# Hybrid SSD and attention layer: a gate vector turned on TensorE and loaded during the up projection, and another order of the last squares, means and scalings

## The chip, the cores and the metric

The kernel runs on one core of one Trainium2 chip. The metric is the time of one execution in microseconds on the device. The engines are named as in the profile: PE is TensorE (PEld its weight loads), DVE is VectorE, ACT is ScalarE, POOL is GpSimd, SP is SyncE. SP issues nearly all transfers in this kernel, and its queue is worked off in order: an issue that has to wait for a semaphore holds all issues behind it.

## The reference, cut to what matters

One layer over 512 latent tokens of width 1024 (and 256 context tokens, which only feed the mixers). The end of it is what the change touches:

```
x = x + gt1 * o_lat                                  # after the token mixer
x = x + gt2 * conv_ffn(modulate(x, norm2_g, sh2, sc2), ...)
return rmsnorm(x, final_g)                           # per token, times final_g per channel

def conv_ffn(h, w_up, conv_w, conv_b, w_down):
    u = dwconv_centred(h @ w_up, conv_w, conv_b)     # 1024 -> 2 x 2816
    return (silu(a) * b) @ w_down                    # 2816 -> 1024
```

gt2 is the last of six modulation vectors of 1024 values, computed from `silu(c) @ w_mod + b_mod`. It multiplies the output of the down projection channel by channel.

## The kernel before, in words

**Precision by three products.** Every weight and operand is split into a high part (whi, `S.copy` on ACT, L181) and a low part (wlo, a subtraction on DVE, L182), and every product is three matmuls (high x high, low x high, high x low). Weights come as pieces of 128 x 1024 values (512 KB), called keys: `load_raw` (L175) loads one to a buffer (tag raw, three of them, or dnraw, four), `split` makes the two parts in one of two buffers each of whi and wlo, or in dnw for two of every four down keys.

**The program.** `run` takes a list of steps with the keys that each needs, loads some keys ahead and emits the step. The instructions are then ordered on each engine by a list scheduler with costs of its own; it may emit an instruction well before its place in the program if what it needs is there. Inside `tc.manual_schedule` the named engines keep the written order. `weave(a, b)` spreads the entries of b evenly between those of a.

**Modulation turns.** The 32 `msteps` compute the modulation vectors beside other work: each scales and adds a weight piece on DVE into a tile tm, and each fourth one turns the sums on TensorE (L793) and adds up eighths of `mod2` (L795, L796). The last eight of them, `msteps[24:]`, are woven between the 22 steps of the up projection; mod2[:, 24:32] is the vector gt2.

**Up projection.** `up_step(t)`, t from 0 to 21, makes two products of 24 matmuls each and the convolution and gate on DVE and ACT. Beside the up steps, `x1_turn` turns the residual stream into rows by token (tiles te) and stores it to x1_d, and `x1_load` reads it back as rows: F["xt"].

**Row vectors.** `row_tiles` brings gt2 (half of it negated) and final_g to row form, so that every one of the 128 partitions holds the whole vector: gt2 lies in `g2c` as 128 partitions x 8, is stored to the DRAM tensor `g2_d` with the pattern "(c p) -> p c", and is read back with `partition_broadcast` into the two tiles rows_["g"]; final_g is read the same way into rows_["f"], whose second half is the tile tm. It is called at the first step of the down projection.

**Down projection.** Seven products, j = 0 to 6, of up to six steps u each, with operands fs of two halves; the weights of j = 1 to 4 are sums that were formed in DRAM earlier (dsum), those of j = 0, 5 and 6 come from wdn. Products 0, 2, 4 and 6 accumulate in two banks F["A"] (name mis), the others in acc. `BESIDE_DOWN` names what runs beside the steps: it forms the four output tiles from the products. The two upper ones (called far) are finished before the last step.

**The end.** The last step (`tail`) makes the product of tile 0, then that of tile 1 in two halves of 256 columns. For each tile and half, `near_last` multiplies by gt2 and adds the residual on DVE and sums the squares on ACT (`square_sum`, output to a buffer of tag ta, of which there are three; near_last takes another of them for its own product). `near_root` adds three partial means and takes the power -0.5: for tile 0 all on GpSimd, for tile 1 the addition on DVE (`mean_root`). `near_out` scales the columns 0 to 511 on ACT (already multiplied by final_g, tile p1, tag tb), scales the two halves of the columns 512 to 1023 on DVE, and issues the stores.

Of the kernel before, what the change touches and what calls it, by code (L numbers as in the profile page):

```python
# [9 lines left out]
F32 = mybir.dt.float32  # L10
F32R = mybir.dt.float32r
U8 = mybir.dt.uint8
AF = mybir.ActivationFunctionType
ALU = mybir.AluOpType
# [4 lines left out]
P = 128  # L19
# [5 lines left out]
NFF = 22  # L25
# [19 lines left out]
def tile_hybrid_layer(  # L45
# [31 lines left out]
    nc = tc.nc  # L77
    V, S, G, T = nc.vector, nc.scalar, nc.gpsimd, nc.tensor

    cpool = ctx.enter_context(tc.tile_pool(name="cpool", bufs=1))  # L80
# [26 lines left out]
    def accb():  # L107
        return bank("acc")

    def misb():  # L110
        return bank("mis")
# [3 lines left out]
    def tmp(tag):  # L115
        return tpool.tile([P, 512], F32, tag=tag, name=tag, bufs=TMP[tag])
# [24 lines left out]
    HC = D // 2  # L141
    DU = (DK + 1) // 2
    DSUMS = {i: dpool.tile([P, DK * HC], F32, name="dsum%d" % i) for i in (1, 2, 4, 5)}
    for j, t in enumerate((wdn[0], DSUMS[1], DSUMS[2], DSUMS[5], DSUMS[4], wdn[1], wdn[3])):
        for u in range(DU):
            n = min(2, DK - 2 * u) * HC
# [69 lines left out]
    def weave(a, b):  # L216
        r, n, m = [], len(a), len(b)
        for i in range(n):
            r.append(a[i])
            r += b[i * m // n : (i + 1) * m // n]  # L220
        return r
# [17 lines left out]
    ident = cpool.tile([P, P], F32, name="ident")  # L239
# [8 lines left out]
    phalf = cpool.tile([P, 4], F32, name="phalf")  # L248
# [15 lines left out]
    g2_d = dpool.tile([D], F32, name="g2_d")  # L264
# [154 lines left out]
    with tc.tile_pool(name="spool", bufs=1) as sp:  # L419
# [235 lines left out]
        r = {}  # L655
        cq = tmp("te")[:, :LC]
        for j in range(KT):
# [46 lines left out]
            x = ("hi", "lo") if j >= NU else ("hh", "hl")  # L704
# [31 lines left out]
        for n in range(2):  # L736
            for j in range(KT):
                x = ("hi", "lo") if j >= NU else ("hh", "hl")
# [131 lines left out]
    Q, F = {}, {}  # L870
# [775 lines left out]
    msteps = [m_step(i) for i in range(32)]  # L1646
    prog = proj_steps(0)
    for g in range(4):
        s = ssd_steps(g)
        f = fill[n2 + g : n2 + 1 + g]  # L1650
        b = proj_steps(g + 1) if g < 3 else fill[n2 + 4 : n3]
# [259 lines left out]
    def up_step(t):  # L1911
        def fn(wa, wb):
            pa, pb = accb(), accb()
            if t == 0:

                with tc.manual_schedule(engines={mybir.EngineType.PE}):
                    def product(ps, w, k, u):
                        c, z, st, en = slice(k * P, (k + 1) * P), HALF[u], u == 0 and k == 0, k == KT - 1
                        for v, y in ((0, h2h), (1, h2h), (0, h2l)):
                            T.matmul(  # L1920
                                ps[:, z], w[v][:, c], y[:, k, z],
                                start=st and v == 0 and y is h2h, stop=en and y is h2l, skip_group_check=True,
                            )

                    for k in range(KT):
                        norm2_k(k, 0)
                        if k == 2:
                            F["rs2"] = half_root(F["pf"], F["sq2"], 1)
                        if k == 5:
                            F["r2"].append(rms_spread(F["rs2"], 2))  # L1930
                        product(pa, wa, k, 0)
                        product(pb, wb, k, 0)
                    for k in range(KT):
                        norm2_k(k, 1)
                        product(pa, wa, k, 1)
                        product(pb, wb, k, 1)
                a = up_first(pa, pb, t)
            else:
                gemm([(pa, h2h, h2l)], wa)
                a = up_first(pa, pb, t)  # L1940
                gemm([(pb, h2h, h2l)], wb)
            up_second(a, pb, t)

        return [("up", t), ("up", NFF + t)], fn

    def x1_turn(c):

        def fn():
            t = tmp("te")
            V.transpose(t, x1[c // 4][:, c % 4, :])  # L1950
            for a in range(4):
                o = x1_d[:, c * P + 32 * a : c * P + 32 * a + 32].rearrange("(f i) j -> i f j", i=32)
                nc.sync.dma_start(o, t[32 * a : 32 * a + 32, :].rearrange("i (f j) -> i f j", j=32))

        return [], fn
# [10 lines left out]
    x1_rows = [], x1_load  # L1966
# [3 lines left out]
    rows_ = {}  # L1970

    def row_tiles():
        V.tensor_copy(g2c[:, 0:4], mod2[:, 24:28])
        V.tensor_scalar_mul(g2c[:, 4:8], mod2[:, 28:32], -1.0)
        nc.sync.dma_start(g2_d.rearrange("(c p) -> p c", p=P), g2c)
        tiles = [hpool.tile([P, HC], F32, tag=t, name="row" + t) for t in ("q2", "ssq", "rbc4")] + [tmp("tm")]
        rows_["g"], rows_["f"] = tiles[:2], tiles[2:]
        for i in range(2):
            z = slice(HC * i, HC * i + HC)
            nc.sync.dma_start(rows_["f"][i], fg_d[z].partition_broadcast(P))  # L1980
            nc.sync.dma_start(rows_["g"][i], g2_d[z].partition_broadcast(P))
# [9 lines left out]

        return F["xt"][h][:, i, HC * c + z.start : HC * c + z.stop]

    def square_sum(h, i, col_, x):
        sq = tmp("ta")[:, : x.shape[-1]]
        S.activation(sq, x, AF.Square, scale=1.0 / 32.0, accum_out=ss[:, 2 * h + i, col_ : col_ + 1])

    def scale_add(x, y, g, h, i, c):
# [37 lines left out]
    def mean_root(h, i, a, b, e):  # L2036
        ms, rs = (cpool.tile([P, 4], F32, tag=n, name=n, bufs=2)[:, 0:1] for n in ("ms", "rs"))
        V.scalar_tensor_tensor(ms, a, e, b, ALU.add, ALU.add)
        G.tensor_tensor(rs, ms, phalf[:, 0:1], ALU.pow)
        return rs  # L2040
# [26 lines left out]
    def near_last(i, b):  # L2067
        z, t = HALF[b], tmp("ta")[:, :HL]
        V.tensor_tensor(t, F["A"][i][:, z], rows_["g"][1][:, z], ALU.mult)
        x = xq(0, i, 1, z)  # L2070
        V.tensor_tensor(x, x, t, ALU.add)
        square_sum(0, i, 1 + b, x)

    def near_root(i):
        if i:
            F["near", i] = mean_root(0, i, ss[:, i, 1:2], ss[:, i, 2:3], ss[:, i, 0:1])
        else:
            ms, rs = (cpool.tile([P, 4], F32, tag=n, name=n, bufs=2)[:, 0:1] for n in ("ms", "rs"))
            G.tensor_tensor(ms, ss[:, i, 0:1], ss[:, i, 1:2], ALU.add)
            G.tensor_tensor(ms, ms, ss[:, i, 2:3], ALU.add)  # L2080
            G.tensor_tensor(rs, ms, phalf[:, 0:1], ALU.pow)
            F["near", i] = rs

    def near_out(i):
        rs, r = F["near", i], P * i
        S.activation(F["p1"][i], F["p1"][i], AF.Copy, scale=rs)
        (S if i else nc.sync).dma_start(out[r : r + P, 0:HC], F["p1"][i])
        for z in HALF:
            x = xq(0, i, 1, z)
            V.scalar_tensor_tensor(x, x, rs, rows_["f"][1][:, z], ALU.mult, ALU.mult)  # L2090
            if i or z.start:
                z = z if i else slice(0, HC)
                nc.sync.dma_start(out[r : r + P, HC + z.start : HC + z.stop], xq(0, i, 1, z))

    CHAIN = (0, 2, 4, 6)
    BESIDE_DOWN = {
        (0, 0): row_tiles, (1, 0): first_kept, (2, 0): fifth_kept, (3, 0): upper_sums, (4, 0): upper_put,
        (4, 4): lambda: far_done(0), (5, 0): lower_put, (5, 5): lambda: (far_done(1), far_roots()), (6, 0): near_put,
        (6, 1): lambda: far_out(0), (6, 2): lambda: far_out(1), (6, 3): near_done,
    }  # L2100
# [13 lines left out]
    def down_step(j, u):  # L2114
        tail = j == 6 and u == DU - 2

        def fn(*w):
            w = {u + n: x for n, x in enumerate(w)}
            if u == 0:
                if j == 0:  # L2120
                    F["A"] = [misb() for _ in TWO]
                F["ps", j] = F["A"] if j in CHAIN else [accb() for _ in TWO]
            ks = range(2 * u, DK if tail else min(2 * u + 2, DK))
            if tail:
                product(j, 0, w, ks)
                for z in HALF:
                    product(j, 1, w, ks, z)
                with tc.manual_schedule(engines={mybir.EngineType.DVE, mybir.EngineType.Activation}):
                    near_last(0, 0), near_last(0, 1)
                    near_root(0), near_last(1, 0), near_last(1, 1), near_root(1)  # L2130
                    near_out(0), near_out(1)
                return
            for k in ks:
                for i in TWO:
                    product(j, i, w, (k,))
            if 1 <= j < 6 and u < 4:
                z = slice(3 * u, min(3 * u + 3, DK))
                f_split((j + 1) % 2, z, OPERAND[j + 1]()[:, z, :])
            BESIDE_DOWN.get((j, u), lambda: None)()

        return [("dn", DU * j + u + n) for n in range(1 + tail)], fn
# [7 lines left out]
        + weave([out_step(o) for o in range(5)], msteps[18:24])  # L2149
        + [([], vectors)]  # L2150
        + [([("out", o) for o in (5, 6, 7)], out_last), ([], close_c1)]
        + weave(weave([up_step(t) for t in range(NFF)], msteps[24:]), [([], lambda: None)] * 6 + [x1_turn(c) for c in range(8)] + [x1_rows] + [([], lambda: None)] * 7)
        + [down_step(j, u) for j in range(7) for u in range(DU - (j == 6))],
        early=("g", 15),
    )
# [85 lines left out]
```

## Time and profile before

| | us |
|---|---|
| median of 3 runs | 1225.65 (1225.18 to 1226.07) |
| profiled execution, its own time | 1227.91 |
| its span | 1226.1 |
| PE busy | 1213.5 (99%) |
| DVE busy | 919.2 (75%) |
| ACT busy | 683.4 (56%) |
| POOL busy | 196.6 (16%) |

The rows in the prediction come from the profile of this one execution. A row of a timeline has the start in us from the span's start, the duration, the engine, the line of the kernel, the operation, the tile written and the tiles read; in brackets stands how long the engine was idle before it and what released it (SPq and ACTq are the queues that issue transfers). A row of the waits says who waited for whom, us in total, how often, and the longest. A row of the chain of waits has start, duration and what it was. A row of the transfers has the destination and source, the queue, how many, the size of one, and the median us from issue to landing. A row of the windows has the stretch and its length, the busy us of PE, PEld, DVE, ACT and POOL with their instructions, then the granted TensorE clock (1.00 is full), the busy share of the DMA engines and the GB/s that they moved. A row of one line's instructions gives the shortest, median and longest in ns, and the first and last start.

### The profile page before, as it was taken

What the parts mean: (1) busy time and instruction counts of PE and PEld (TensorE: products, weight loads), DVE (VectorE), ACT (ScalarE), POOL (GpSimd) and SP (SyncE); (2) the same over time, 40 slices, a digit from 0 to 9 for tenths busy, and PEclk for the clock granted to TensorE, in tenths of its full rate; (3) what the DMA queues carried; (4) which work ended last, traced back from release to release, by engine and by line L of the source; (5) the groups of instructions that cost most, each with busy time, mean ns of one, the idle gap of its engine ahead of it and who ended that gap; (6) DMA issues with size and microseconds to landing.
All of it is one profiled execution on the core that took longest, in us unless ns stands there. A gap on an engine that the chain in (4) does not pass through costs nothing.

```text
span 1226.1 us, 17441 instructions
## 1 busy us (share of the span) xinstructions
PE 1213.5 (99%) x6319; PEld 996.9 (81%) x6319; DVE 919.2 (75%) x1480; ACT 683.4 (56%) x1275; POOL 196.6 (16%) x189
## 2 busy tenths in 40 slices
PE   9999999999999999999999999999999999999997
PEld 6798888888878878778777778889988888887885
DVE  5857787888554598697896767677887877776776
ACT  5658788787444467486574663223644443445653
POOL 0000121101000044352552630000200000000043
PEclk9999999999999999999999999999999999999999
DMA  9645799844755336346366568676356433348752
GB/s 369 256 136 183 159 249 257 170 154 124 174 160 149 129 103 175 113 130 194 106 173 203 163 213 266 225 256 208 70 135 187 146 116 105 103 136 196 245 177 87
DMA packets 122407, 211.55 MB, mean 173 GB/s; under 512 B 26704, under 2 KB 68752, under 8 KB 122320
## 3 DMA queue, kind: packets, MB, share of 16 engines
q1 hardware_dynamic: 111280, 187.09, 49.3%
q0 software_dynamic: 10752, 23.07, 8.5%
q8 instruction: 50, 0.82, 0.3%
q14 instruction: 37, 0.30, 0.1%
q10 hardware_dynamic: 288, 0.27, 0.1%
HBM read 185.68 MB, written 42.28 MB: 186 GB/s over the span
## 4 chain that ended last, share of the span: by engine, by line
PE 94%; DMA 2%; ACT 1%; DVE 1%; issue 1%; POOL 0%; POOLq 0%; DVEq 0%; ACTq 0%; SPq 0%
PE acc L231 20%; PE acc L234 19%; PE acc L232 19%; PE score L951 3%; PE po L1000 3%; PE mis L573 2%; PE pt L987 2%; PE mis L1604 2%; PE mis L1497 2%; PE mis L1612 1%; PE acc L2112 1%; PE acc L2110 1%; PE acc L2111 1%; PE acc L1070 1%; PE mis L2112 1%; PE mis L2110 1%
## 5 line engine op out<-in xcount | busy, mean ns | idle before, releaser
L181 ACT CAST whi<-wraw 128x1024 fp32r<-128x1024 f32 (+1 forms) x115 | 120.3, 1047 | 152.3 <-PE acc L232 110.2
L182 DVE TENSOR_TENSOR wlo<-wraw,whi 128x1024 fp32r<-128x1024 f32 (+1 forms) x115 | 144.5, 1256 | 66.5 <-ACT whi L181 62.3
L231 PE MATMUL acc<-hlh,whi 128*128 128x512 f32 x472 | 194.2, 411 | 0.0
L232 PE MATMUL acc<-hll,whi 128*128 128x512 f32 x472 | 184.9, 392 | 0.0
L234 PE MATMUL acc<-hlh,wlo 128*128 128x512 f32 x472 | 184.9, 392 | 0.0
L231 PE MATMUL acc<-mh,whi 128*128 128x512 f32 x368 | 143.4, 390 | 0.0
L232 PE MATMUL acc<-ml,whi 128*128 128x512 f32 x368 | 143.2, 389 | 0.0
L234 PE MATMUL acc<-mh,wlo 128*128 128x512 f32 x368 | 143.2, 389 | 0.0
L234 PEld LDWEIGHTS acc<-hlh,wlo 128*128 128x128 f32 x472 | 88.6, 188 | 19.5
L231 PEld LDWEIGHTS acc<-hlh,whi 128*128 128x128 f32 x472 | 88.8, 188 | 17.9 <-issue 3.1
L232 PEld LDWEIGHTS acc<-hll,whi 128*128 128x128 f32 x472 | 88.9, 188 | 17.4 <-issue 2.4
L234 PEld LDWEIGHTS acc<-mh,wlo 128*128 128x128 f32 x368 | 69.1, 188 | 14.5
L231 PEld LDWEIGHTS acc<-mh,whi 128*128 128x128 f32 x368 | 69.1, 188 | 14.4
L232 PEld LDWEIGHTS acc<-ml,whi 128*128 128x128 f32 x368 | 69.1, 188 | 14.1
L1385 DVE SCALAR_TENSOR_TENSOR ta<-acc,half,ta 128x511 f32<-128x511 f32 (+1 forms) x66 | 43.9, 665 | 27.2 <-ACT ta L1384 26.9
L960 DVE CUSTOM_DVE_ANT_0 p<-score,winm,nsink 128x512 f32<-128x512 f32 (+1 forms) x64 | 51.9, 811 | 15.3 <-PE score L951 13.8
L1384 ACT ACTIVATE ta<-acc,half 128x512 f32<-128x512 f32 (+1 forms) x66 | 46.9, 711 | 22.0 <-PE acc L234 20.7
L967 ACT ACTIVATE p<-p,mneg 128x512 f32<-128x512 f32 (+1 forms) x64 | 49.7, 777 | 15.4 <-DVE mneg L960 14.8
L162 POOL DMA_DIRECT2D dsum<-wdn x24 | 25.4, 1143 | 193.7 <-DVE wlo L1084 172.4
L1499 POOL TENSOR_TENSOR st<-st,eT 128x512 f32<-128x512 f32 x24 | 29.7, 1236 | 165.5 <-ACT st L1516 151.9
L231 PE MATMUL acc<-hch,whi 128*128 128x256 f32 x176 | 54.7, 311 | 0.0
L995 DVE TENSOR_TENSOR ptl<-pt,pth 128x512 fp32r<-128x512 f32 x72 | 47.5, 686 | 9.2 <-ACT pth L991 7.7
(429 smaller groups left out, 3006.3 us busy)
## 6 DMA issues: line engine op xcount, KB each, us to landing
wraw<-wup SPq DMA_DIRECT2D x44, 512.0 KB, 3.6
dsum<-wdn POOLq DMA_DIRECT2D x24, 704.0 KB, 8.7
fb<-cs_d SPq DMA_DIRECT2D x32, 512.0 KB, 6.6
wraw<-wm SPq DMA_DIRECT2D x32, 512.0 KB, 3.8
wraw<-wx SPq DMA_DIRECT2D x24, 512.0 KB, 3.5
wm<-wm SPq DMA_DIRECT2D x16, 512.0 KB, 8.1
wraw<-wz SPq DMA_DIRECT2D x16, 512.0 KB, 4.0
wraw<-wos SPq DMA_DIRECT2D x16, 512.0 KB, 4.6
```

What stands on the lines that cost most here:

```text
L181: S.copy(hi[:, :n], r[:, :n])
L182: return V.tensor_tensor(lo[:, :n], r[:, :n], raw(hi[:, :n]), ALU.subtract)
L231: T.matmul(ps, wh, xh[:, k0 + k, :], start=a, stop=False)
L232: T.matmul(ps, wh, xl[:, k0 + k, :], start=False, stop=False)
L234: T.matmul(ps, wl, xh[:, k0 + k, :], start=False, stop=b)
L951: T.matmul(ps[:, o : o + len(z) * P], Q[h][:, b * P : (b + 1) * P], k[:, j, z[0] * P : (z[-1] + 1) * P], start=v == 0 and o % 512 in (0, P ...
L960: V.tensor_tensor_reduce(p[:, :w], d["ps"][i][:, o0 : o0 + w], m, op0=ALU.add, op1=ALU.min, scale=1.0, scalar=nsink[:, h : h + 1], accum_o ...
L967: S.activation(p, p, AF.Exp, bias=d["mneg"][:, i : i + 1], scale=-1.0, accum_out=d["den"][:, i : i + 1])
L995: V.tensor_tensor(d["ptl"][x], d["pt"][x], raw(d["pth"][x]), ALU.subtract)
L1000: T.matmul(d["po"], vst[:, cols[x], j, :], d[y][x], start=x == 0 and y == "pth", stop=x == c - 1 and y == "ptl")
L1384: S.activation(o[:, :n], ps[:, :n], AF.Identity, scale=hcol(base_w, stride + i), bias=hcol(base_b, i))
L1385: V.scalar_tensor_tensor(o[:, 1:n], ps[:, 0 : n - 1], hcol(base_w, i), o[:, 1:n], ALU.mult, ALU.add)
```

## The change

The gate vector is turned from 128 x 8 to 8 x 128 with one transpose on TensorE, copied out of the bank on DVE to a tile te, and stored with the pattern "(c p) -> c p". `row_tiles` leaves the first step of the down projection and stands after the 20th up step; for that the last eight modulation turns are woven between the first 18 up steps and not between all 22. At the end the squares of `near_last` go to buffers of tag te and no longer ta; both tiles' means are added on GpSimd; and `near_out` becomes two functions, with the second half of tile 0 scaled on DVE ahead of the others, and its store ahead on SP.

```diff
--- before.py
+++ after.py
@@ -1972,7 +1972,10 @@
     def row_tiles():
         V.tensor_copy(g2c[:, 0:4], mod2[:, 24:28])
         V.tensor_scalar_mul(g2c[:, 4:8], mod2[:, 28:32], -1.0)
-        nc.sync.dma_start(g2_d.rearrange("(c p) -> p c", p=P), g2c)
+        ps, t = misb(), tmp("te")
+        T.transpose(ps[0:8, 0:P], g2c, ident)
+        V.tensor_copy(t[0:8, 0:P], ps[0:8, 0:P])
+        nc.sync.dma_start(g2_d.rearrange("(c p) -> c p", p=P), t[0:8, 0:P])
         tiles = [hpool.tile([P, HC], F32, tag=t, name="row" + t) for t in ("q2", "ssq", "rbc4")] + [tmp("tm")]
         rows_["g"], rows_["f"] = tiles[:2], tiles[2:]
         for i in range(2):
@@ -1991,8 +1994,8 @@
 
         return F["xt"][h][:, i, HC * c + z.start : HC * c + z.stop]
 
-    def square_sum(h, i, col_, x):
-        sq = tmp("ta")[:, : x.shape[-1]]
+    def square_sum(h, i, col_, x, tag="ta"):
+        sq = tmp(tag)[:, : x.shape[-1]]
         S.activation(sq, x, AF.Square, scale=1.0 / 32.0, accum_out=ss[:, 2 * h + i, col_ : col_ + 1])
 
     def scale_add(x, y, g, h, i, c):
@@ -2069,32 +2072,31 @@
         V.tensor_tensor(t, F["A"][i][:, z], rows_["g"][1][:, z], ALU.mult)
         x = xq(0, i, 1, z)
         V.tensor_tensor(x, x, t, ALU.add)
-        square_sum(0, i, 1 + b, x)
+        square_sum(0, i, 1 + b, x, "te")
 
     def near_root(i):
-        if i:
-            F["near", i] = mean_root(0, i, ss[:, i, 1:2], ss[:, i, 2:3], ss[:, i, 0:1])
-        else:
-            ms, rs = (cpool.tile([P, 4], F32, tag=n, name=n, bufs=2)[:, 0:1] for n in ("ms", "rs"))
-            G.tensor_tensor(ms, ss[:, i, 0:1], ss[:, i, 1:2], ALU.add)
-            G.tensor_tensor(ms, ms, ss[:, i, 2:3], ALU.add)
-            G.tensor_tensor(rs, ms, phalf[:, 0:1], ALU.pow)
-            F["near", i] = rs
-
-    def near_out(i):
-        rs, r = F["near", i], P * i
-        S.activation(F["p1"][i], F["p1"][i], AF.Copy, scale=rs)
-        (S if i else nc.sync).dma_start(out[r : r + P, 0:HC], F["p1"][i])
+        ms, rs = (cpool.tile([P, 4], F32, tag=n, name=n, bufs=2)[:, 0:1] for n in ("ms", "rs"))
+        G.tensor_tensor(ms, ss[:, i, 0:1], ss[:, i, 1:2], ALU.add)
+        G.tensor_tensor(ms, ms, ss[:, i, 2:3], ALU.add)
+        G.tensor_tensor(rs, ms, phalf[:, 0:1], ALU.pow)
+        F["near", i] = rs
+
+    def near_first(i):
+        S.activation(F["p1"][i], F["p1"][i], AF.Copy, scale=F["near", i])
+        (S if i else nc.sync).dma_start(out[P * i : P * i + P, 0:HC], F["p1"][i])
+
+    def near_second(i):
+        r = P * i
         for z in HALF:
             x = xq(0, i, 1, z)
-            V.scalar_tensor_tensor(x, x, rs, rows_["f"][1][:, z], ALU.mult, ALU.mult)
+            V.scalar_tensor_tensor(x, x, F["near", i], rows_["f"][1][:, z], ALU.mult, ALU.mult)
             if i or z.start:
                 z = z if i else slice(0, HC)
                 nc.sync.dma_start(out[r : r + P, HC + z.start : HC + z.stop], xq(0, i, 1, z))
 
     CHAIN = (0, 2, 4, 6)
     BESIDE_DOWN = {
-        (0, 0): row_tiles, (1, 0): first_kept, (2, 0): fifth_kept, (3, 0): upper_sums, (4, 0): upper_put,
+        (1, 0): first_kept, (2, 0): fifth_kept, (3, 0): upper_sums, (4, 0): upper_put,
         (4, 4): lambda: far_done(0), (5, 0): lower_put, (5, 5): lambda: (far_done(1), far_roots()), (6, 0): near_put,
         (6, 1): lambda: far_out(0), (6, 2): lambda: far_out(1), (6, 3): near_done,
     }
@@ -2126,9 +2128,9 @@
                 for z in HALF:
                     product(j, 1, w, ks, z)
                 with tc.manual_schedule(engines={mybir.EngineType.DVE, mybir.EngineType.Activation}):
-                    near_last(0, 0), near_last(0, 1)
-                    near_root(0), near_last(1, 0), near_last(1, 1), near_root(1)
-                    near_out(0), near_out(1)
+                    near_last(0, 0), near_last(0, 1), near_root(0)
+                    near_last(1, 0), near_last(1, 1), near_root(1)
+                    near_second(0), near_first(0), near_first(1), near_second(1)
                 return
             for k in ks:
                 for i in TWO:
@@ -2149,7 +2151,10 @@
         + weave([out_step(o) for o in range(5)], msteps[18:24])
         + [([], vectors)]
         + [([("out", o) for o in (5, 6, 7)], out_last), ([], close_c1)]
-        + weave(weave([up_step(t) for t in range(NFF)], msteps[24:]), [([], lambda: None)] * 6 + [x1_turn(c) for c in range(8)] + [x1_rows] + [([], lambda: None)] * 7)
+        + weave(
+            weave([up_step(t) for t in range(18)], msteps[24:]) + [up_step(t) for t in range(18, NFF)],
+            [([], lambda: None)] * 6 + [x1_turn(c) for c in range(8)] + [x1_rows] + [([], lambda: None)] * 4 + [([], row_tiles)] + [([], lambda: None)] * 2,
+        )
         + [down_step(j, u) for j in range(7) for u in range(DU - (j == 6))],
         early=("g", 15),
     )
```

## The prediction

> **What bounds the kernel now.** I read the busy times first, then the waits of PE from the start of the up projection on, then the timeline of PE where its one gap lies, then the queue and the transfers behind that gap, and last the timeline of the tail.
>
> ```profile
> PE 1213.5 (99%) x6319; PEld 996.9 (81%) x6319; DVE 919.2 (75%) x1480; ACT 683.4 (56%) x1275; POOL 196.6 (16%) x189
> PE acc L2110 <- ACT dnw L181: 1.4, 1, 1.4
> PE acc L2112 <- DVE dnw L182: 0.5, 1, 0.5
> ```
>
> PE is the bound nearly everywhere. From 860 us to the end it waits for other engines in two places only, and both belong to one event: the first weights of the second down product (stage j = 1, tile dnw). So there are two things the change can win: that one gap, and the tail behind PE's last matmul. Everything it adds elsewhere is free unless PE waits for it. The gap:
>
> ```profile
> 1118.88 0.39 PE L2112 MATMUL mis<-dnw,fs 128*128 128x512 f32 x1
> 1122.95 0.39 PE L2112 MATMUL mis<-wlo,fs 128*128 128x512 f32 x1
> 1124.78 0.50 PE L2110 MATMUL acc<-dnw,fs 128*128 128x512 f32 x1 [1.43 <-ACT dnw L181]
> 1126.03 0.80 PE L2112 MATMUL acc<-dnw,fs 128*128 128x512 f32 x1 [0.52 <-DVE dnw L182]
> 1129.42 0.40 PE L2111 MATMUL acc<-dnw,fs 128*128 128x512 f32 x1
> 1126.00:1128.00 2.00, 1.97 (x5) 1.58 (x6) 2.00 (x3) 2.00 (x4) 0.00 (x0) 0.50 0.72 173
> ```
>
> Between the first two rows lie 18 steps in 4.07 us, a pitch of 0.226 us. The last matmul of stage 0 starts at 1122.95. Counted in the cycle of its three lines (L2110, L2111, L2112), the row at 1126.03 is the third of the next stage and the row at 1129.42 the eleventh. Undisturbed, the eleventh would start 11 x 0.226 = 2.49 us after 1122.95; it starts 6.47 us after. **The gap costs 3.98 us.** Its parts: the first three steps take 3.08 instead of 0.68 us (2.40 lost to waiting), the next eight take 3.39 instead of 1.81 us (1.58 lost), and in those the granted clock is 0.50 (last figure but two of the window row).
>
> Why the weights are late:
>
> ```profile
> 1112.08 11.50 DMA wraw<-dsum
> 1123.68 1.04 ACT L181 CAST dnw<-wraw 128x1024 fp32r<-128x1024 f32 x1 [6.41 <-DMA wraw<-dsum]
> 1112.82 0.38 SPq L1975 DMA_DIRECT2D g_d<-g2c  x1
> 1125.48 0.32 SPq L1981 DMA_DIRECT2D rowq<-g_d  x1
> 1126.88 0.32 SPq L175 DMA_DIRECT2D wraw<-dsum  x1
> g_d<-g2c SPq DMA_DIRECT2D x1, 4.0 KB, 12.6
> wraw<-dsum SPq DMA_DIRECT2D x12, 512.0 KB, 5.4
> 1112.00:1114.00 2.00, 2.00 (x11) 1.65 (x10) 2.00 (x5) 0.84 (x1) 0.00 (x0) 1.00 0.97 365
> 1118.00:1120.00 2.00, 2.00 (x10) 1.66 (x9) 0.60 (x2) 0.00 (x0) 0.00 (x0) 1.00 0.96 68
> 1120.00:1122.00 2.00, 2.00 (x10) 1.68 (x9) 0.00 (x0) 0.00 (x0) 0.00 (x0) 1.00 0.63 45
> ```
>
> The 512 KB of the first weights of stage 1 are issued at 1112.08 and land 11.5 us later; twelve loads of that kind have a median of 5.4. In between, at 1112.82, the store of the gate vector goes out: 4 KB, written element by element (128 partitions to a column order), and it takes 12.6 us. The windows show its mark: with the DMA engines equally busy (0.97 and 0.96), 365 GB/s fall to 68. SP, which must see that store landed before it reads the vector back, holds everything behind L1981 until 1125.48.
>
> **The change, part by part.**
>
> *The store by rows.* The vector is turned on TensorE to 8 rows of 128, and the store writes 8 runs of 512 bytes instead of 1024 elements. The same step is emitted after the 20th up step instead of the first down step, for which the last modulation turns move into the first 18 up steps. So at 1112 neither the store nor the two row loads stand in the queue, and the weight load needs what its like need. At 5.4 us it lands at 1117.5. Stage 1 could start at 1123.18; ahead of it lie the cast (1.04 us) and the subtraction, so landing by 1121.3 is early enough, and 3.8 us are in hand. ACT and DVE are free for it (0.00 and 0.60 us busy in the window from 1118, nothing after), and the last matmul that reads the earlier dnw starts at 1118.88, so its buffer is free too. All of 3.98 us goes, the slow clock included, since without the gap PE is never idle there. Next late in that place: nothing before the 1121.3; the later weights gain, because SP no longer holds the load of 1126.88.
>
> *What it adds to PE.* One transpose of 128 x 8, out through 128 columns.
>
> ```profile
> 1107.89 0.45 PE mis L793 x4
> out<-tb ACTq DMA_DIRECT2D x1, 256.0 KB, 3.2
> 1075.05 1.05 ACT L181 CAST whi<-wraw 128x1024 fp32r<-128x1024 f32 x1 [0.16 <-PE acc L232]
> 1076.14 1.23 DVE L182 TENSOR_TENSOR wlo<-wraw,whi 128x1024 fp32r<-128x1024 f32 x1 [0.52 <-ACT whi L181]
> 1080.49 1.06 ACT L181 CAST whi<-wraw 128x1024 fp32r<-128x1024 f32 x1 [0.52 <-PE acc L232]
> ```
>
> Four transposes of 128 x 128 take 0.45 us of the chain, so one is 0.11 us. It also waits for the vector on DVE; its program place is two up steps after the last turn (some 22 us: two keys a step, 5.44 us a key by the last two casts of these rows), so I take 0.1 us for that, with bounds of 0 and 1.2 us (one subtraction standing ahead on DVE). Behind a waiting transpose stand all of PE's matmuls, so that is a real price. The two small DVE copies lie under PE's matmuls. Together 0.2 us.
>
> *The new place on SP.* SP waits for the store before it issues the row loads; behind it stand weight loads of the up projection and the first down weights. The landing is bounded below by nothing much and above by 3.2 us (the slowest plain store above) or, if something goes wrong, by the 12.6. Headroom: each cast waits for PE to release one of two buffers, so a key cast at 1075.05 is needed when the next is released, 1080.49; its subtraction ends at 1077.37. That is 3.1 us to spare even there, where the cast followed its load without slack. 3.2 against 3.1 with the worst of both: cost nothing, bound 1.5 us. The row loads and the broadcast of final_g are moved past the same queue, 3 x 256 KB in a stretch without a PE wait.
>
> *The tail.* Behind PE's last matmuls:
>
> ```profile
> 1216.46 0.43 DVE L2071 TENSOR_TENSOR xt<-xt,ta 128x256 f32<-128x256 f32 x1
> 1217.24 0.18 ACT L1996 ACTIVATION_READ_ACCUMULATOR ta<-xt 128x1 f32 x1
> 1217.43 0.42 DVE L2069 TENSOR_TENSOR ta<-mis,rowssq 128x256 f32<-128x256 f32 x1 [0.54 <-ACT ta L1996]
> 1217.57 0.19 POOL L2080 TENSOR_TENSOR ms<-ms,ss 128x1 f32<-128x1 f32 x1 [0.54 <-ACT ta L1996]
> 1217.84 0.55 POOL L2081 TENSOR_TENSOR rs<-ms,phalf 128x1 f32<-128x1 f32 x1
> 1218.68 0.42 DVE L2071 TENSOR_TENSOR xt<-xt,ta 128x256 f32<-128x256 f32 x1
> 1219.52 0.19 ACT L1996 ACTIVATION_READ_ACCUMULATOR ta<-xt 128x1 f32 x1
> 1219.74 0.22 DVE L2038 SCALAR_TENSOR_TENSOR ms<-ss 128x1 f32<-128x1 f32 x1 [0.64 <-ACT ta L1996]
> 1220.04 0.72 POOL L2039 TENSOR_TENSOR rs<-ms,phalf 128x1 f32<-128x1 f32 x1 [1.65 <-DVE ms L2038]
> 1219.88 1.80 DVE L2090 SCALAR_TENSOR_TENSOR xt<-xt,rs,tm 128x256 f32<-128x256 f32 x4
> 1221.08 1.54 SPq L2093 DMA_DIRECT2D out<-xt  x3
> L2039 POOL TENSOR_TENSOR rs<-ms,phalf x3: 557/725/937, 1197.2 to 1220.0; 128x1 f32<-128x1 f32 x3
> ```
>
> DVE and the squares on ACT share the three buffers of ta, and at 1216.89 DVE waits 0.54 us for a square to release one. Squares in te remove that, and the second tile's sums, the last square and its accumulator read come 0.54 us earlier (read done at 1219.17 instead of 1219.71). From the read to the root the first tile's way on GpSimd takes 1218.39 - 1217.42 = 0.97 us, the second tile's way over DVE 1220.76 - 1219.71 = 1.05: another 0.08. Scaling the first tile ahead fills DVE from about 1218.6 to 1219.5, where it used to wait; it takes its two operations of 0.45 out of the time before the second root, but the second tile's end hung on that root anyway, so it wins nothing by itself. The second tile's two scalings and the last stores on SP follow the root: 0.62 us earlier in all.
>
> Against it: GpSimd's tiny operations now run beside DVE's scalings. The same pow took 0.56 to 0.94 us, against 0.55 for L2081, so 0.39 us is the most that row gives for being beside DVE; the tail then wins 0.23. The first tile's scalings end (1219.5) about when the deciding add starts, so I take 0.6. The Trainium skill ("SBUF — State Buffer", section "Who interferes with whom") says a DVE instruction with two SBUF inputs and a GpSimd instruction that reads SBUF exclude each other for a whole instruction; by it the first small add would sit behind the first tile's scalings until 1219.5 and the root come some 0.1 us later, an estimate that leaves 0.5.
>
> **Sum.** 3.98 + 0.6 - 0.2 = 4.4 us. The profiled span of 1226.1 becomes 1221.7, its own time of 1227.91 becomes 1223.5, and the median of the runs, 1225.65, which lies 2.26 below the profiled execution, becomes **1221.2 us**. This kernel's measurement can tell about 0.2% from no change, 2.45 us, so the limits are 1223.2 and 1228.1.
>
> **Rivals.**
>
> *The slow clock stays.* If the 0.50 has another cause than the gap, only the 2.40 goes: 2.40 + 0.6 - 0.2 = 2.8, 1222.9 us. For it: PE stood still for only 1.43 + 0.52 us, with two matmuls between. Against it: the clock is 1.00 in every window up to 1122 and drops just behind the gap. Chance 0.04. The Trainium skill ("TensorE: Matmul & The Clock Gate", section "What's actually happening") lets the clock fall after an idle window of about 3.4 us; read strictly, that speaks for this rival, but the windows counted are the chip's own and the row shows the fall.
>
> *The load is late anyway.* Several weight loads are issued within 6 us and the DMA engines are full at 1112; if their load and not the 4 KB store delays the first one, the gap stays and only the tail is won: 1225.65 - 0.4 = 1225.2, no change. Against it: 68 GB/s at the same busy share is no queue of 512 KB loads. Chance 0.06. A change that does not do what it says (the step placed late after all, since the instructions are ordered by a planner) ends here too.
>
> *SP is held in the up projection (slower).* The order on SP is fixed before the run. If the store is put well ahead of the moment its vector is ready, SP stands at it with weight loads behind. What decides is a hold over some 3 to 8 us (the 3.1 above, or one more key of 5.44 where no modulation load comes between). A hold of 15 us, less 5 of headroom, plus 1.6 of slow clock, loses 11.6 against 4.4 won: 1232.9 us. For it: the gap of the kernel before is a misplaced wait of just this kind, 10 us long. Against it: its vector is ready some 20 us ahead of its program place. Chance 0.05. A short hold or a wait of the transpose, 1 to 2.5 us lost, ends between 1222.2 and 1223.7: chance 0.07, half of it faster.
>
> **How the numbers follow.** The forecast has 0.78. Faster: 0.78 + 0.04 + 0.05 = 0.87. Same: 0.06 and the rest of the short holds, 0.08. Slower: 0.05. The range reaches from 1219.9 (the tail a little better, the later loads too) to 1223.3, which takes in the slow-clock case and the bounds of the transpose and SP.
>
> **What would show it.** Right: no PE wait for dnw near 1120, the granted clock 1.00 throughout the down projection, the first dsum load landed in about 5 to 6 us, the gate vector's store in some 2 to 3 us in the up projection, no DVE wait for ACT's ta in the tail, the pow on GpSimd about 0.6 us nearer to PE's last matmul. Wrong: a PE wait in the up projection at the transpose or at whi, or the dnw wait still there without the 4 KB store.

## The result and the profile after

The changed kernel takes 1222.88 us (median of 22 runs, 1222.54 to 1223.57), the kernel before 1224.56 us (22 runs on the same chip, 1223.23 to 1228.64): a ratio of 0.9984 with the interval 0.9979 to 0.999, 1.7 us less. The profiled execution went from 1227.91 us to 1223.03, its span from 1226.1 to 1221.2: 4.9 us less. The two differences do not agree, and most of the experiments are about that.

First the profile of the changed kernel at the places that the prediction showed: busy times, PE's timeline where the gap was, the cast of the first summed weights, the queue, one group of transfers, and windows.

```profile
PE 1211.1 (99%) x6320; PEld 995.6 (82%) x6320; DVE 921.1 (75%) x1480; ACT 683.1 (56%) x1275; POOL 196.3 (16%) x191
1122.33 0.39 PE L2114 MATMUL mis<-wlo,fs 128*128 128x512 f32 x1
1122.56 0.39 PE L2112 MATMUL acc<-dnw,fs 128*128 128x512 f32 x1
1111.70 0.33 SPq L175 DMA_DIRECT2D wraw<-dsum  x1
1116.96 1.05 ACT L181 CAST dnw<-wraw 128x1024 fp32r<-128x1024 f32 x1 [1.53 <-DMA wraw<-dsum]
wraw<-dsum SPq DMA_DIRECT2D x7, 512.0 KB, 5.0
1085.48 0.39 PE L234 MATMUL acc<-mh,wlo 128*128 128x512 f32 x1
1085.71 0.27 PE L1976 MATMUL mis<-ident,g2c 128*8 128x128 f32 x1
1086.29 0.39 PE L234 MATMUL acc<-mh,wlo 128*128 128x512 f32 x1
1086.33 0.34 SPq L1978 DMA_DIRECT2D g_d<-te  x1
1088.42 1.28 SPq L1984 DMA_DIRECT2D rowq<-g_d  x1
1118.00:1120.00 2.00, 2.00 (x10) 1.66 (x9) 1.96 (x2) 1.69 (x3) 0.00 (x0) 1.00 1.00 337
1126.00:1128.00 2.00, 2.00 (x11) 1.65 (x9) 1.66 (x2) 1.67 (x3) 0.00 (x0) 1.00 0.88 346
```

Stage 1 of the down projection follows stage 0 at PE's pitch of 0.23 us; the waits of PE from 860 us on are an empty list. The first summed weights are issued at 1111.70 and their cast starts at 1116.96, right at the landing: 5.3 us, and 5.6 before PE uses them. The window from 1118 moves 337 GB/s where it moved 68. The transpose is one matmul at 1085.71; three steps of 0.226 us behind 1085.48 would be at 1086.16, and the third matmul besides the transpose starts at 1086.29, 0.13 us later. The store by rows has landed by 1088.42, when SP issues the row load that waits for it. The clock stays 1.00.

The tail of the changed kernel:

```profile
1212.41 0.28 PE L2114 MATMUL mis<-wlo,fs 128*128 128x256 f32 x1
1212.73 0.42 DVE L2072 TENSOR_TENSOR ta<-mis,rowssq 128x256 f32<-128x256 f32 x1 [0.46 <-PE mis L2114]
1214.82 0.19 ACT L1999 ACTIVATION_READ_ACCUMULATOR te<-xt 128x1 f32 x1
1215.42 0.55 POOL L2081 TENSOR_TENSOR rs<-ms,phalf 128x1 f32<-128x1 f32 x1
1216.00 0.88 DVE L2092 SCALAR_TENSOR_TENSOR xt<-xt,rs,tm 128x256 f32<-128x256 f32 x2 [0.81 <-POOL rs L2081]
```

Two rows of the kernel before, PE's last matmul and the scaling of the second tile:

```profile
1217.04 0.28 PE L2112 MATMUL mis<-wlo,fs 128*128 128x256 f32 x1
1220.80 0.72 ACT L2086 ACTIVATE tb<-tb,rs 128x512 f32<-128x512 f32 x1 [0.48 <-POOL rs L2039]
```

DVE no longer waits for ACT to release ta. It waits instead for PE's very last matmul, 0.46 us in place of 0.54. From the start of that matmul to the second tile's scaling it is 1216.00 - 1212.41 = 3.59 us; before it was 1220.80 - 1217.04 = 3.76 (ACT's scaling, released by the same root as DVE's; in the changed kernel ACT's too starts at 1216.00). From the same point to the end of the span it is 8.79 us and was 9.06.

So of the 4.9 us between the two spans 0.3 lie in the tail; PE's last matmul starts 4.63 us earlier, and the gap of 3.98 is nearly all of that (the stages before the down projection ended 0.48 earlier in this execution; that moment differs between executions, from 1107.03 to 1108.67 in the runs below).

### The profile page after: what moved, and what is told of

The parts are those of the page before. It is cut to its first block, busy times and chain, and to the rows that moved or that the text cites. A ratio compares the mean times of both kernels' runs of the same rounds, so it can differ in the third digit from the quotient of the medians.

```text
span 1221.2 us, 17447 instructions
## 1 busy us (share of the span) xinstructions
PE 1211.1 (99%) x6320; PEld 995.6 (82%) x6320; DVE 921.1 (75%) x1480; ACT 683.1 (56%) x1275; POOL 196.3 (16%) x191
## 4 chain that ended last, share of the span: by engine, by line
PE 97%; issue 1%; DVE 1%; ACT 0%; DMA 0%; POOL 0%; POOLq 0%; DVEq 0%; ACTq 0%
PE acc L231 20%; PE acc L234 20%; PE acc L232 20%; PE score L951 3%; PE po L1000 3%; PE pt L987 2%; PE mis L573 2%; PE mis L1604 2%; PE mis L1497 2%; PE mis L2113 2%; PE mis L2114 2%; PE mis L2112 2%; PE mis L1612 1%; PE acc L2112 1%; PE acc L2113 1%; PE acc L2114 1%
```

## Experiments

**How long is the gap in other executions?** Two theories for the 1.7 us against 4.9: the gap of the profiled execution was that execution's, or the changed kernel loses time where its profile did not show it. The unchanged kernel was run again, twice.

> The unchanged kernel once more. Theory A: the 3.98 us gap before the second down product was that one execution's; what the store of the gate vector costs differs from execution to execution, and in an ordinary execution of 1224.5 us it is 1 to 1.5 us. Then this profile shows another length of the gap, and its own time is the 1223 us of the changed kernel plus that gap plus about 0.3. Theory B: the gap is about 4 us in every execution, and the changed kernel gives 2.7 us back in a place its profile has not shown; then the gap is 4 us here too, whatever the time.

> The unchanged kernel a third time. If the gap differs by execution, its length here is once more another one (0.2 to 4.2 us), and the execution's own time less the gap is 1223.3 to 1224.4, as it was in the two before.

The first: 1224.49 us (12 runs, 1222.96 to 1228.10), ratio 1.0 with the interval 0.9989 to 1.0011; the profiled execution took 1226.55. The second, one execution: 1227.64. Rows of the first, then of the second (the two waits at the start of stage 1, first matmul of stage 0, last matmul, one window):

```profile
1124.84 0.50 PE L2110 MATMUL acc<-dnw,fs 128*128 128x512 f32 x1 [0.91 <-ACT dnw L181]
1126.10 0.50 PE L2112 MATMUL acc<-dnw,fs 128*128 128x512 f32 x1 [0.53 <-DVE dnw L182]
1108.67 0.49 PE L2110 MATMUL mis<-whi,fs 128*128 128x512 f32 x1
1215.62 0.28 PE L2112 MATMUL mis<-wlo,fs 128*128 128x256 f32 x1
1126.00:1128.00 2.00, 1.90 (x8) 1.59 (x9) 2.00 (x4) 2.00 (x3) 0.00 (x0) 1.00 0.39 130
```

```profile
1124.30 0.50 PE L2110 MATMUL acc<-dnw,fs 128*128 128x512 f32 x1 [1.62 <-ACT dnw L181]
1125.56 0.67 PE L2112 MATMUL acc<-dnw,fs 128*128 128x512 f32 x1 [0.53 <-DVE dnw L182]
1107.41 0.49 PE L2110 MATMUL mis<-whi,fs 128*128 128x512 f32 x1
1216.68 0.28 PE L2112 MATMUL mis<-wlo,fs 128*128 128x256 f32 x1
1126.00:1128.00 2.00, 2.00 (x6) 1.58 (x5) 2.00 (x3) 2.00 (x4) 0.00 (x0) 0.50 0.72 162
```

From the first matmul of stage 0 to the last of the kernel the changed kernel takes 104.81 us (1107.60 to 1212.41). The kernel before took 108.96 (1108.08 to 1217.04), 106.95 and 109.27 in its three profiles: excesses of 4.15, 2.14 and 4.46. Their own times less the excess are 1223.76, 1224.41 and 1223.18. The last is just outside what was expected of it (an excess up to 4.2, 1223.3 to 1224.4). Three kernels of the experiments below also make the element-wise store once in the old place, and their profiles have excesses of 4.22 (rows_by_pool, an execution of 1227.50 us), 1.07 (tail_only, 1223.64) and 0.15 (pool_store, 1224.82). So the gap differs from execution to execution, and with it the time of the kernel, though not the gap alone: pool_store's execution has almost none and its stage 0 starts late, at 1108.53. The clock is part of the gap: after waits of 0.91 and 0.53 us it stayed at 1.00, after 1.62 and 0.53 and after 1.43 and 0.52 it fell to 0.50, and the excess is 2 us larger.

**The shape of the store or its place?** Each alone, with the tail of before.

```diff
 # turn_only: in the old place (first down step)
-        nc.sync.dma_start(g2_d.rearrange("(c p) -> p c", p=P), g2c)
+        ps, t = misb(), tmp("te")
+        T.transpose(ps[0:8, 0:P], g2c, ident)
+        V.tensor_copy(t[0:8, 0:P], ps[0:8, 0:P])
+        nc.sync.dma_start(g2_d.rearrange("(c p) -> c p", p=P), t[0:8, 0:P])
 # place_only: the element-wise store stays, row_tiles and the last turns move as in the change
```

> The vector is turned on TensorE and stored by rows, but in the old place (first down step), and the tail is as before. If the element-wise store is what fills the transfer engines (theory of the prediction), the store lands in 2 to 3 us, the first summed weights in 5 to 6 us, and the wait for dnw is gone: 1223.2 us, about 1.4 below the kernel before. If the place in the queue costs as much (rival), a wait of 1 us or more for dnw stays and the time is within 0.5 us of the kernel before.

> The new place in the up projection, but the store element by element and the tail as before. If the shape alone matters, the 10 to 13 us store now holds SP in the up projection; the headroom there (3 us, or 8 where no modulation load comes between) decides: a hold of 10 us would show as a wait of PE for whi of 2 to 4 us, time at or over the kernel before. If the headroom is larger, since the last up weights are issued before and the first down weights are wanted only 18 us later, there is no wait and the time is 1223.2 us.

turn_only: 1223.49 us, ratio 0.999 (0.9981 to 0.9998); one of its 12 executions took 2467.19 us, about twice the others, which no run explains, and the median of the other eleven is 1223.40. place_only: 1223.43 us (1223.06 to 1224.07), ratio 0.999 (0.9982 to 0.9999). Neither profile has a wait of PE behind 860 us. Rows of turn_only, then of place_only:

```profile
1113.69 0.34 SPq L1978 DMA_DIRECT2D g_d<-te  x1
1116.88 1.06 ACT L181 CAST dnw<-wraw 128x1024 fp32r<-128x1024 f32 x1 [0.39 <-DMA wraw<-dsum]
1118.21 0.32 SPq L1984 DMA_DIRECT2D rowq<-g_d  x1
```

```profile
1068.01 0.38 SPq L1975 DMA_DIRECT2D g_d<-g2c  x1
1077.07 0.33 SPq L1981 DMA_DIRECT2D rowq<-g_d  x1
g_d<-g2c SPq DMA_DIRECT2D x1, 4.0 KB, 9.0
```

Either half of the front is enough. In the old place, stored by rows, the weights land by 1116.88. In the new place the element-wise store takes 9.0 us and holds SP until 1077.07, and PE does not notice. By medians the gap is worth 1224.56 - 1223.46, 1.1 us, which is about the excess in the profile of tail_only (1.07 us), an execution 0.8 us below its kernel's median, whose front is that of the kernel before; its wait for dnw, 0.54 us, comes later in stage 1, at 1134.67. I take this for the ordinary execution's gap. Theory B falls with the excesses of 2.14 and 1.07.

**What about the store costs the time?** Three variants of the kernel before: the row loads issued by GpSimd, so that SP is not held; the store and the row loads by GpSimd, so that the elements use another queue; the store made twice. And the changed kernel with an additional store of the same elements 512 bytes apart.

```diff
 # rows_by_pool (and pool_store, where the store is G.dma_start too)
-            nc.sync.dma_start(rows_["g"][i], g2_d[z].partition_broadcast(P))
+            G.dma_start(rows_["g"][i], g2_d[z].partition_broadcast(P))
 # double_store: one line more, ahead of the store
+        nc.sync.dma_start(g3_d.rearrange("(c p) -> p c", p=P), g2c)
 # wide_store, on the changed kernel; g4_d is [D, 128], read by nobody
+        nc.sync.dma_start(g4_d.rearrange("(c p) e -> p c e", p=P)[:, :, 0:1], g2c.rearrange("p (c e) -> p c e", e=1))
```

> The kernel before, but the two row loads of the gate vector are issued by GpSimd, which is idle there, so that SP does not stand at the landing of the element-wise store. Theory (the 1024 elements fill the rings that the weight loads use): the store still lands in about 12 us, the first summed weights still in 9 to 12, the wait for dnw stays at 1 to 4 us in the profile and the time stays at 1224.5. Rival (the hold of SP is the cost): the wait goes and the time is 1223.2 us.

> The kernel before, with the element-wise store and the two row loads issued by GpSimd, so that the 1024 elements go through another queue of the same 16 transfer engines. If the elements hurt because they stand in the same rings in front of the weight loads, the first summed weights land in 5 to 6 us and the time is 1223.2 to 1223.5. If they hold the engines themselves, whichever queue they come from, the load still takes 8 to 12 us and the time is 1224.5.

> The kernel before with the element-wise store made twice in the old place (the other time to a DRAM tensor that nobody reads). If the store is the cause, its cost doubles at least: the transfers behind it lie still for another 8 to 12 us, most of which is not covered any more, 1231 to 1236 us. If the gap in the kernel before has another cause, the time stays within 1.5 us of it.

> The changed kernel with an additional store of the same 1024 elements of 4 bytes in the up projection, each to a row of its own 512 bytes apart, in a tensor that nobody reads. The element-wise store to neighbouring addresses took 9.0 us in that quiet place. If each element costs its time, this one takes 9 us too. If neighbours in one line of the memory wait for each other, as two stores at once taking no longer than one suggests, it takes 3 to 4 us. The time of the kernel does not change in either case (1222.9), as nothing waits for it but the row store behind it in the queue.

rows_by_pool: 1226.12 us, ratio 1.0008 (0.9996 to 1.0021), a median above the forecast 1224.5, but not told apart from the kernel before. pool_store: 1224.35, ratio 1.0007 (0.9998 to 1.0015). double_store: 1225.24, ratio 1.0004 (0.9993 to 1.0016). wide_store: 1221.9 in one execution. Rows of the four in this order:

```profile
1124.00 0.50 PE L2110 MATMUL acc<-dnw,fs 128*128 128x512 f32 x1 [1.56 <-ACT dnw L181]
g_d<-g2c SPq DMA_DIRECT2D x1, 4.0 KB, 11.8
```

```profile
wraw<-dsum SPq DMA_DIRECT2D x6, 512.0 KB, 9.9
g_d<-g2c POOLq DMA_DIRECT2D x1, 4.0 KB, 11.6
```

```profile
g_d<-g2c SPq DMA_DIRECT2D x2, 4.0 KB, 11.7
```

```profile
g_d<-g2c SPq DMA_DIRECT2D x1, 4.0 KB, 3.0
```

SP's hold is not the cost: without it the wait for dnw is there (1.56 us). The queue is not it either: from GpSimd's queue the store takes as long and the weight loads on SP's queue slow down too (the first takes 7.6 us, the median of six is 9.9, where the changed kernel has 5.0); that execution happened to have no wait of PE, and the median stays with the kernel before. The doubled store was a miss: it did not cost 6 us and more, since two stores at once take no longer than one. The spread store goes with that: the same 1024 elements, each 512 bytes from the next, land in 3.0 us, against 9.0 in nearly the same place (1067.31 and 1068.01) when they are neighbours. So, by one execution of each, it is not the number of elements that makes the store long, but that they are written side by side. That neighbours wait for each other in the memory is what I argue from it; no run shows the mechanism. Nor was the spread store made in the old place: whether the weight loads would pass beside it is not shown. Why the same store lets the weights through after some 8 us in one execution (tail_only) and after 11.5 in another stays open.

**The tail.** Alone, with one thing put back at a time, and with the new wait taken away.

```diff
 # tail_only: the kernel before with the change's tail alone
 # ta_back, on the changed kernel
-        square_sum(0, i, 1 + b, x, "te")
+        square_sum(0, i, 1 + b, x)
 # dve_mean, on the changed kernel, first lines of near_root
+        if i:
+            F["near", i] = mean_root(0, i, ss[:, i, 1:2], ss[:, i, 2:3], ss[:, i, 0:1])
+            return
 # own_bank, on the changed kernel, in the last down step
-                for z in HALF:
-                    product(j, 1, w, ks, z)
+                product(j, 1, w, ks, HALF[0])
+                product(j, 1, w, ks, HALF[1], F["own"][:, :HL])   # a bank of acc
 # and ahead of it, so that near_last(1, 1) multiplies F["own"] alone
+        V.tensor_tensor(t, F["A"][1][:, z], rows_["g"][1][:, z], ALU.mult)
+        V.tensor_tensor(x, x, t, ALU.add)
```

> Only the end is changed (squares in te, both means on GpSimd, first tile scaled ahead). The prediction's step gave 0.6 us; the profile of the changed kernel shows 8.79 us from the start of PE's last matmul to the end where the kernel before has 9.06, so 0.27. Expected: 8.8 us from the last matmul's start to the end, and 0.3 us off the time, which the differing gap before may hide.

> The changed kernel with the squares of the end back in the tile ta. The prediction gave the tiles te 0.54 us. Theory now: DVE waits 0.54 for ACT instead of 0.46 for PE, so te is worth 0.1 us at most: 1222.9 to 1223.0. If te is worth its 0.54: 1223.4 us.

> The changed kernel, but the mean of tile 1 is added on DVE again, ahead of the first tile's scalings, as in the kernel before. The kernels with the new front and the old tail measure 1223.43 and 1223.49, the changed kernel 1222.88, and te is worth 0.08 of that. Theory: the rest, 0.4 us, comes with the mean off DVE, since the first tile is then scaled and stored while the second waits for its root, and the last stores are less crowded; expected 1223.3. If the rest belongs to the order of the functions alone or to nothing of the tail: 1222.9 to 1223.0.

> The changed kernel, with one thing in the tail different: the last three steps of the second half of tile 1 go to a bank of their own, and what that half has so far is multiplied and added to the residual ahead (two more DVE operations of 0.42 us). Theory: with te for the squares the first half of tile 1 on DVE waits for PE's very last matmul, though its own last matmul is 1.08 us earlier, since both halves share one bank; then it now starts right behind DVE's own work, the wait of 0.46 us for PE goes, and 0.2 to 0.5 us come off: 1222.5 us. Rival: the wait is only inferred and something else holds DVE; then the two added operations cost up to 0.3 us, 1223.1 us.

tail_only: 1224.41 us, ratio 1.0003 (0.9993 to 1.0013): the differing gap hides it, and the profile has 8.58 us from the last matmul's start to the end of the span. ta_back: 1222.96 (0.9988, 0.9979 to 0.9996). dve_mean: 1223.07 (0.9989, 0.998 to 0.9998). own_bank: 1222.46 us (11 runs, 1221.90 to 1223.12), ratio 0.9984 (0.9975 to 0.9992). The rows of ta_back, then of dve_mean, then of own_bank:

```profile
1212.40 0.28 PE L2114 MATMUL mis<-wlo,fs 128*128 128x256 f32 x1
1212.78 0.43 DVE L2072 TENSOR_TENSOR ta<-mis,rowssq 128x256 f32<-128x256 f32 x1 [0.54 <-ACT ta L1999]
1216.06 0.88 DVE L2092 SCALAR_TENSOR_TENSOR xt<-xt,rs,tm 128x256 f32<-128x256 f32 x2 [0.81 <-POOL rs L2081]
```

```profile
1212.45 0.28 PE L2117 MATMUL mis<-wlo,fs 128*128 128x256 f32 x1
1216.13 0.72 ACT L2088 ACTIVATE tb<-tb,rs 128x512 f32<-128x512 f32 x1 [0.47 <-POOL rs L2042]
```

```profile
1212.56 0.28 PE L2121 MATMUL acc<-wlo,fs 128*128 128x256 f32 x1
1212.34 0.42 DVE L2073 TENSOR_TENSOR ta<-mis,rowssq 128x256 f32<-128x256 f32 x1
1215.61 0.88 DVE L2099 SCALAR_TENSOR_TENSOR xt<-xt,rs,tm 128x256 f32<-128x256 f32 x2 [0.77 <-POOL rs L2088]
```

These kernels ran on different chips: the kernel before took 1224.56 us where tail_only ran, 1224.21 where ta_back and own_bank ran, and 1223.81 where dve_mean ran. So a few tenths between two of these medians show nothing by themselves, and the intervals of the ratios of ta_back, dve_mean, own_bank and the changed kernel overlap (own_bank's ratio and the changed kernel's are both 0.9984).

The profiles are steadier. From the start of PE's last matmul to the scaling of the second tile it is 3.76 us in six profiles with the old tail (4.11 and 4.12 in rows_by_pool and pool_store) and 3.59 in all three with the new one (the changed kernel, tail_only, wide_store). With ta in place of te it is 3.66: the tiles te are worth 0.07. With the mean back on DVE it is 3.68: taking it off is worth 0.09. With a bank of its own for the second half, DVE takes up the first half before PE's last matmul has even started, and it is 3.05, 0.54 less; that its median of 1222.46 is below the changed kernel's for this reason is not shown.

Behind that scaling's start lie the last stores. From there to the end of the span it is 5.3 to 5.4 us in the eight profiles with the old tail, 5.3 in dve_mean, and 4.3 to 5.2 in the five where the mean is on GpSimd and the first tile is scaled ahead. So this order wins some tenths there; that it does so because the stores are less crowded is argued, and how much differs between executions (5.2 us in the changed kernel's, 4.3 in wide_store's, whose time of 1221.9 is so short for that).

## Why the prediction held where it did, and where it did not

The predicted 1221.2 us was 1.7 below the measured 1222.88, which lies in the range (1219.9 to 1223.3). The forecast 4.4 us of gain was 1.7, and with 0.16% the result falls within the 0.2% for which the prediction gave a chance of 0.08, not into the 0.87 of faster. (That 0.87 counts 0.05 of the 0.07 for the short holds, where the text says half.) That the time itself lies in the range is in part luck: the sum started from 1225.65, the median of three runs, and by 22 runs the kernel before takes 1224.56. From there 4.4 us lead to 1220.2, 2.7 us below the measured time; a base 1.1 too high made up for part of a gain 2.7 too large.

- *The gap and its cause.* Right in the profile: the wait is gone, the weights land in 5.3 us (5.4 taken), the clock stays at 1.00, nothing else became late. By the other runs the slow clock belongs to the gap, so the rival of the slow clock falls, and so does the rival of the load that is late anyway (turn_only). One part of the reason was wrong as it stands: the long store was laid to the writing element by element. wide_store shows as many elements landing in 3.0 us.
- *The sum.* This is the step that failed. It took 3.98 us from one execution, and then let the median, "which lies 2.26 below the profiled execution", move by the same amount. Those 2.26 us (3.35 against the median of 22) were no constant offset; they were for the larger part the gap itself, which was longer in the profiled execution than in the ordinary one. Kernels without a gap show none: the profiled execution of the changed kernel is 0.15 us above its median, those of turn_only, place_only, ta_back, dve_mean and own_bank lie between 0.4 below and 0.3 above theirs. The gap's term for the median is 1.1 us (turn_only and place_only), and 1.1 + 0.55 is the measured 1.7. The clue lay in the numbers shown: an execution 2.26 above the median of runs that agree within 0.9 had to have something that they did not have.
- *The transpose and SP.* 0.2 us was allowed; the transpose set the matmuls behind it back by 0.13 us, about the 0.11 taken for it, and no wait shows. SP's new place cost nothing, as taken; place_only shows that even a hold of 9 us there costs nothing, so the headroom of 3.1 us was too small a bound for that place, and the slower rival is further off than its price said.
- *The tail.* 0.6 was forecast and 0.55 came by the medians (1223.43 for place_only, 1222.88), but not by the steps named, so that the sum agrees is luck. The 0.54 for te was 0.07: the removed wait had another right behind it, of 0.46, for PE's last matmul. own_bank removes that wait; whether DVE waited because both halves lie in one bank or because they are one tile to the program, it does not tell apart. The last matmul of the kernel before ended, at 1217.04 + 0.28, 0.1 us before the start that DVE was seen to wait for. The mean off DVE was to give 0.08 and gave 0.09. The slowing of GpSimd beside DVE that was allowed for did not touch the path: the first tile's pow took 0.80 us in the changed kernel, but the deciding one, which ran while DVE waited for it, 0.55. The scaling ahead was said to win nothing by itself; together with the mean off DVE it wins the rest, behind the second scaling, where the prediction's sum had no term. How much of the 0.55 that is, the profiles bound only roughly: 0.17 comes before.

## What to carry to other kernels

Before a stall is priced from a profile, ask how the profiled execution stands to the median of the runs: an execution that is well above it may hold a longer stall than the others, and the stall's length in it is no term for the median. For each wait that is removed, look for the next event that the waiting instruction needs; here it came 0.08 us earlier than the one removed. A small transposing store is better turned on chip first, or at least issued where the queue is quiet: either was enough.

## What the runs showed of the hardware

Two things were not expected. A store of 1024 elements of 4 bytes took 9.0 us in a quiet stretch and 11.6 to 12.7 beside weight loads when its elements were neighbours in memory, with two of them at once no slower, and 3.0 us when each stood 512 bytes from the next; a 512 KB load issued just ahead of it took 7.6 to 11.7 us, and 4.8 to 5.7 where no such store ran beside it. And TensorE's granted clock fell to 0.50 after a standstill of 1.43 us followed by another of 0.52 (also after 1.62 and 0.53), but not after 0.91 and 0.53. The Trainium skill ("TensorE: Matmul & The Clock Gate", section "What's actually happening") puts the fall behind an idle window of about 3.4 us; in these traces a shorter standstill was enough.
